# A list schedule that orders a hybrid decoder layer's instructions: port locks, matmul issue times and narrow DMAs enter its model

## The chip, the core and the metric

The kernel runs on one core of a Trainium2 chip. The metric is device time in microseconds (us) of one execution; lower is better. The engines are named as in the profile: PE is TensorE's matmuls and PEld its weight loads, DVE is VectorE, ACT ScalarE, POOL GpSimd, SP the engine whose queue issues all DMAs here.

## The reference

One decoder layer over 2048 tokens of width 1024 in float32, with two groups of heads side by side:

```python
h = rmsnorm(x, norm_w) * (1 + scale) + shift          # scale, shift, gate from c @ w_ada
mq, mk, mv, mo, mz, mi, mf, aq, ak, av, az = split(h @ w_in)
mq, mk = silu(causal_dwconv(mq)), silu(causal_dwconv(mk))
hm = sigmoid(mo) * head_layernorm(mlstm_chunkwise(mq, mk, mv, mi, log_sigmoid(mf))) * silu(mz)
...
logits = q @ k.T + rel_bias[t5_bucket]                # two softmax maps per head, causal
w = softmax(logits_0) - lam * softmax(logits_1)
ha = rmsnorm(w @ v, a_norm_w) * (1 - lam_init) * silu(az)
y = concatenate([hm, ha]) @ w_out
out = rmsnorm(x + gate * y, final_norm_w)
```

The mLSTM group has 4 heads of 256, the attention group 8 heads with two 64-wide query/key maps and 128-wide values.

## The kernel before, in words

Every float32 operand of a large product is split into two parts, `hi` and `lo`, that TensorE reads in its faster float32 form; a product is three matmuls (hi·hi, hi·lo, lo·hi). The split costs one ACT copy (hi) and one subtraction on DVE or POOL (lo). So weights, projected activations, attention weights and the mLSTM state all pass ACT and then DVE or POOL before PE may use them.

`build` (L270) notes the program in this order: `load_x`, `adaln` and `make_h` (normalised tokens), `phase_a` (L721, attention projections of one half of the tokens), `attention` (L798) for the first half, `phase_a` and `attention` for the second, `phase_m` (L940, mLSTM projections), `mlstm` (L1043) for chunks 0 to 7 of 128 tokens, `phase_m` and `phase_zo` for the second half, `mlstm` for chunks 8 to 15, `out_proj` (L1142). Projections, attention maps and states go through DRAM (`dQ`, `dK`, `dV`, `dMK` and so on); all DMAs are issued from SP's queue.

None of these calls issues anything. A `Lane` notes each call in `Program.ops` with the earlier instructions it depends on (`note`, L166). At the end `order` (L195) makes a list schedule: it keeps a modelled time at which each of the five engines is free, gives the engine that is free first the earliest noted instruction whose operands are modelled to be there, and adds the instruction's modelled cost (`cost`, L141) and a latency between engines (`AFTER`). `issue` (L240) then issues everything in that order, so all lines of the profile are L243, and each engine runs its instructions strictly in the order found. The model's times decide nothing but this order. Thus PE gets matmuls of a later projection (`ps_pj`) as filler wherever the model says that the next matmul of the current stage is not ready yet.

```python
if ins[0].dtype == F32R:
    return max(108.0, 3 + n / 2.4)                        # L148, ns
...
if method in ("tensor_scalar", "tensor_copy") and "PSUM" not in str(ins[0].space):
    return 68.0 + n * 0.53                                # L161
```

Three places matter below. In `mlstm`, at the end of a chunk, DVE combines the denominators (`sm`), POOL raises them to the power -1/2 (L1128), DVE normalises the four heads with one `tensor_scalar` each from SBUF to SBUF (`hn`, L1131), and PE transposes each result (L1135). In `attention`, a head begins with two loads of its keys into `Kt`, partitions 0 to 63 and 64 to 127, which may start when the last score matmul (`ps_S`) of the head before has read the old keys. And between the transposes of attention weights (`ps_tr`) and their product with the values (`ps_pv`) stand the ACT copy and the DVE subtraction of the split.

Of the kernel before, what the change touches and what calls it, by code (L numbers as in the profile page):

```python
# [13 lines left out]
PSUM = bass.MemoryType.PSUM  # L14
DRAM = bass.MemoryType.DRAM
# [54 lines left out]
class Lane:  # L70
    """One engine's instruction stream: calls are noted down, not issued."""

# [9 lines left out]
class Program:  # L82
    """Notes the kernel's instructions with what they read and write, then issues them in the
    order of a list schedule: whenever an engine is free it takes the first noted instruction
    whose operands are there."""

# [54 lines left out]
    def cost(self, lane, method, out, ins, kwargs):  # L141
        n = self.width(out)
        if lane == "sync":
            return 530.0
        if lane == "tensor":
            if method == "transpose":
                return 109.0
            if ins[0].dtype == F32R:  # L148
                return max(108.0, 3 + n / 2.4)
            return 2 * max(108.0, 3 + n / 1.2)  # L150
        if lane == "scalar":
            aps = sum(isinstance(kwargs.get(k), bass.AP) for k in ("scale", "bias", "accum_out"))
            return 51.0 + n / 1.2 + 93.0 * aps
        n = max(n, max((self.width(a) for a in ins), default=0))
        if lane == "gpsimd":
            if kwargs.get("op") == ALU.pow:
                return 300.0 + 165.0 * n
            return 150.0 + n * (2.1 if method == "tensor_tensor" else 0.9)
        scalars = [a for a in ins if self.width(a) == 1]
        if method in ("tensor_scalar", "tensor_copy") and "PSUM" not in str(ins[0].space):  # L160
            return 68.0 + n * 0.53  # L161
        if method == "reciprocal":
            return 60.0 + n * 8
        return 68.0 + n * 1.042 + (62.0 if scalars else 0.0)

    def note(self, lane, method, args, kwargs):  # L166
        rest = list(args)
        out = kwargs["out"] if "out" in kwargs else rest.pop(0)
# [4 lines left out]
        deps = set()  # L173
# [15 lines left out]
        if self.hold is not None:  # L189
            deps.add(self.hold)  # L190
        size = 4.0 * self.width(out) * out.shape[0]
        self.ops.append((lane, method, args, kwargs, self.cost(lane, method, out, ins, kwargs),
                         deps, k - self.ahead, size))

    def order(self):  # L195
# [9 lines left out]
        free = {n: 0.0 for n in self.LANES}  # L205
        dma = 0.0
        for k, o in enumerate(ops):
            if left[k] == 0:
                heapq.heappush(soon[o[0]], (0.0, k))
        done = []  # L210
        while len(done) < len(ops):
# [10 lines left out]
            while soon[lane] and soon[lane][0][0] <= best:  # L222
                k = heapq.heappop(soon[lane])[1]
                heapq.heappush(now[lane], (ops[k][6], k))
            k = heapq.heappop(now[lane])[1]
            o = ops[k]
            end = best + o[4] * (2 if lane == "tensor" and best < self.COLD else 1)
            free[lane] = end
            if lane == "sync":
                dma = max(dma, best + 1400.0) + o[7] / 350.0  # L230
                end = dma + 1000.0
# [14 lines left out]
class K:  # L246
# [174 lines left out]

# [1 line left out]
    def ht(self, slot, lo):  # L423
# [5 lines left out]
    def turned(self, n, vecs):  # L429
        """vectors over channels, turned so that channels lie on partitions"""  # L430
        nc = self.nc
# [23 lines left out]
    def adaln(self, g, on_pe):  # L455
        """shift and scale of 256 channels: some of the products on TensorE, the others on VectorE"""
        nc = self.nc
# [30 lines left out]
    def load_x(self, tg):  # L488
        """x of four token tiles, scaled by its reciprocal root mean square"""
        nc = self.nc  # L490
# [41 lines left out]
    def out_gate(self):  # L532
        """the output gate on all partitions, kept in DRAM"""
        nc = self.nc
# [16 lines left out]
    def gate_weights(self):  # L551
        """the gates' columns, beside the last slot of the weight ring"""
        nc = self.nc
# [88 lines left out]

# [1 line left out]
    def fill_w(self, c0, hi, lo, eng=None):  # L644
# [16 lines left out]
    def load_w2(self, c0, *slots):  # L661
        """256 columns in one load: two slots of the ring, or one wide one"""
        nc = self.nc
# [10 lines left out]
    def proj_c(self, w, slot, name):  # L674
        """channel-major block: [128 channels, 512 tokens]"""
        pj = self.psum("pj", name)
        self.proj_k(pj, w, slot, range(KT))
        return pj
# [10 lines left out]
    def proj_t(self, w, slot, j2, name):  # L689
        """token-major block: two tiles of [128 tokens, 256 columns]"""  # L690
        pj = self.psum("pj", name)
        for j in range(2):
            self.proj_r(pj[:, j * 256:(j + 1) * 256], w, slot, 2 * j2 + j)
        return pj
# [81 lines left out]

# [1 line left out]
    def bias_tiles(self):  # L778
# [154 lines left out]

# [1 line left out]
    def stage_m(self):  # L935
# [76 lines left out]

# [1 line left out]
    def mlstm_buffers(self):  # L1014
# [224 lines left out]
```

## Time and profile before

| | |
|---|---|
| time, median of 3 runs | 2996.12 us (2994.66 to 2997.53) |
| profiled execution | span 2997.5 us; it has no time of its own beside the span; the longest of the three times is 2997.53 us |
| busy: PE, PEld | 2849.1 us (95%), 2454.4 us (82%) |
| busy: DVE, ACT, POOL | 1649.4 us (55%), 1351.0 us (45%), 914.4 us (31%) |
| mean granted TensorE clock | 0.980 of full speed |
| DMA | 419.96 MB moved, 140 GB/s in the mean |

The engine table gives the share of the span in which an engine worked; a PE that is 95% busy leaves 148 us of idle time. The windows view cuts this by stage, the waits view says what each idle stretch of PE ended on, and the timeline shows one such place instruction by instruction. A granted clock of 0.50 means 1.2 GHz, of 1.00 means 2.4 GHz.

### The profile page before, as it was taken

What the parts mean: (1) busy time and instruction counts of PE and PEld (TensorE: products, weight loads), DVE (VectorE), ACT (ScalarE), POOL (GpSimd) and SP (SyncE); (2) the same over time, 40 slices, a digit from 0 to 9 for tenths busy, and PEclk for the clock granted to TensorE, in tenths of its full rate; (3) what the DMA queues carried; (4) which work ended last, traced back from release to release, by engine and by line L of the source; (5) the groups of instructions that cost most, each with busy time, mean ns of one, the idle gap of its engine ahead of it and who ended that gap; (6) DMA issues with size and microseconds to landing.
All of it is one profiled execution on the core that took longest, in us unless ns stands there. A gap on an engine that the chain in (4) does not pass through costs nothing.

```text
span 2997.5 us, 43354 instructions
## 1 busy us (share of the span) xinstructions
PE 2849.1 (95%) x16032; PEld 2454.4 (82%) x16032; DVE 1649.4 (55%) x3378; ACT 1351.0 (45%) x3355; POOL 914.4 (31%) x594
## 2 busy tenths in 40 slices
PE   7999999999999999999999999999989889999999
PEld 5878888888888888798887888788788877878887
DVE  6123327776711557766866767866777575232222
ACT  4111325565611455565655656664554454221211
POOL 3112232322312232231221232233544454243332
PEclk9999999999999999999999999999999999999999
DMA  7356667666654632334253335524433444333332
GB/s 257 110 164 231 222 214 218 176 163 176 182 171 123 210 96 87 100 103 115 75 130 84 109 102 190 148 78 123 133 117 98 143 126 150 103 124 115 126 115 97
DMA packets 407539, 419.96 MB, mean 140 GB/s; under 512 B 19540, under 2 KB 348446, under 8 KB 405278
## 3 DMA queue, kind: packets, MB, share of 16 engines
q1 hardware_dynamic: 407326, 417.19, 46.7%
q8 instruction: 126, 2.06, 0.3%
q14 instruction: 87, 0.71, 0.1%
HBM read 280.77 MB, written 136.35 MB: 139 GB/s over the span
## 4 chain that ended last, share of the span: by engine, by line
PE 75%; DVE 10%; DMA 7%; ACT 3%; issue 3%; POOL 2%; SPq 1%; POOLq 0%; DVEq 0%; ACTq 0%
PE ps_pj L243 51%; PE ps_S L243 12%; DVE af L243 7%; PE ps_pv L243 7%; PE ps_tr L243 5%; DMA ar<-dK 3%; ACT af L243 2%; POOL ar L243 1%; ACT ar L243 1%; DVE ar L243 1%; DMA ar<-dQ 1%; SPq L243 1%; DMA af<-in_w_in_dram 1%; DMA ar<-dV 1%; DVE mn L243 1%
## 5 line engine op out<-in xcount | busy, mean ns | idle before, releaser
L243 PE MATMUL ps_pj<-ar 128*128 128x512 f32 (+2 forms) x9936 | 2162.6, 363 | 6.5 <-POOL ar L243 3.1
L243 PEld LDWEIGHTS ps_pj<-ar 128*128 128x128 f32 x9936 | 1648.1, 190 | 268.7 <-issue 5.3
L243 POOL TENSOR_TENSOR ar<-af,ar 128x1024 fp32r<-128x1024 f32 (+3 forms) x308 | 627.9, 2048 | 1068.6 <-ACT ar L243 934.4
L243 PE MATMUL ps_S<-ar 128*128 128x512 f32 (+4 forms) x2096 | 527.6, 357 | 42.3 <-DMA ar<-dK 22.4
L243 ACT ACTIVATE af<-ps_S,nm 128x512 f32<-128x512 f32 (+2 forms) x608 | 386.8, 642 | 141.4 <-DVE nm L243 92.0
L243 ACT ACTIVATE ar<-af 128x1024 fp32r<-128x1024 f32 (+3 forms) x321 | 285.7, 907 | 342.1 <-PE ps_pj L243 201.7
L243 PEld LDWEIGHTS ps_S<-ar 128*128 128x128 f32 x2096 | 351.2, 197 | 91.4 <-issue 33.7
L243 DVE TENSOR_REDUCE mn<-ps_S 128x1 f32<-128x512 f32 (+3 forms) x512 | 297.6, 589 | 146.5 <-PE ps_S L243 143.6
L243 ACT ACTIVATE af<-ps_pj 128x512 f32<-128x512 f32 (+2 forms) x292 | 171.2, 586 | 431.6 <-PE ps_pj L243 385.4
L243 PE MATMUL ps_pv<-ar 128*128 128x256 f32 (+2 forms) x1920 | 319.7, 283 | 20.4 <-DVE af L243 9.2
L243 POOL TENSOR_SCALAR af<-af,rZ,nlam 128x128 f32<-128x128 f32 (+15 forms) x128 | 168.3, 1315 | 529.4 <-DVE rZ L243 445.8
L243 PEld LDWEIGHTS ps_pv<-ar 128*128 128x128 f32 x1920 | 280.5, 190 | 56.7 <-DVE ar L243 16.2
L243 ACT ACTIVATE ar<-ps_tr 128x512 fp32r<-128x512 f32 (+1 forms) x288 | 165.7, 575 | 236.3 <-PE ps_tr L243 226.0
L243 DVE TENSOR_TENSOR ar<-ps_tr,ar 128x512 fp32r<-128x512 f32 (+1 forms) x288 | 188.8, 656 | 113.4 <-ACT ar L243 112.6
L243 DVE SCALAR_TENSOR_TENSOR af<-af,rZ 128x128 f32<-128x128 f32 (+15 forms) x128 | 193.8, 1514 | 27.6 <-POOL af L243 27.3
L243 DVE SCALAR_TENSOR_TENSOR af<-af,cols 128x512 f32<-128x512 f32 x192 | 189.7, 989 | 30.8 <-ACT af L243 28.8
L243 PE MATMUL ps_tr<-ident,af 128*128 128x128 f32 x1115 | 184.8, 277 | 12.9 <-DVE af L243 12.4
L243 DVE TENSOR_TENSOR af<-ps_pj,af 128x512 fp32r<-128x512 f32 (+3 forms) x103 | 66.3, 643 | 186.1 <-ACT af L243 174.7
L243 ACT ACTIVATE af<-af 128x512 f32<-128x512 f32 (+3 forms) x114 | 78.1, 685 | 181.8 <-DVE af L243 176.7
L243 PEld LDWEIGHTS ps_tr<-ident,af 128*128 128x128 f32 x1115 | 134.4, 142 | 26.3 <-DVE af L243 16.5
L243 POOL TENSOR_TENSOR ss<-ss,half 128x2 f32<-128x2 f32 x64 | 48.9, 764 | 337.4 <-DVE ss L243 286.8
L243 DVE TENSOR_TENSOR ps_pj<-ps_pj,af 128x512 f32<-128x512 f32 (+1 forms) x33 | 22.6, 683 | 206.2 <-PE ps_pj L243 206.2
(135 smaller groups left out, 1748.0 us busy)
## 6 DMA issues: line engine op xcount, KB each, us to landing
af<-in_w_in_dram SPq DMA_DIRECT2D x50, 1024.0 KB, 5.1
ar<-dQ SPq DMA_DIRECT2D x128, 256.0 KB, 4.2
af<-in_w_in_dram SPq DMA_DIRECT2D x44, 512.0 KB, 5.0
af<-in_x_dram SPq DMA_DIRECT2D x32, 512.0 KB, 3.8
dQ<-af SPq DMA_DIRECT2D x64, 256.0 KB, 4.8
dK<-af SPq DMA_DIRECT2D x64, 256.0 KB, 3.9
dV<-af SPq DMA_DIRECT2D x64, 256.0 KB, 2.2
dH<-ar SPq DMA_DIRECT2D x32, 512.0 KB, 6.1
```

The lines of the kernel that those rows point to most:

```text
L243: getattr(getattr(nc, lane), method)(*args, **kwargs)
```

## The change

Only the schedule's model changes; the noted instructions, their number and their data are the same. Four edits: a float32-form matmul of n columns costs 13 + n/2.4 ns in place of 3 + n/2.4; a DMA with 64 or fewer partitions on the SBUF side counts 1/0.55 times its bytes against the modelled 350 bytes per ns; a new function `locks` marks the instructions that hold a port pair common to DVE and POOL (POOL's that read SBUF; DVE's copies and `tensor_scalar` from SBUF to SBUF, and DVE's with two wide SBUF inputs); and `order` lets a marked instruction start only when the other engine's last marked one has ended: the engine is put off to that time, and nothing else is taken for it before.

```diff
-                return max(108.0, 3 + n / 2.4)
+                return max(108.0, 13 + n / 2.4)
...
+    def locks(self, lane, method, out, ins):
+
+        near = [a for a in ins if str(a.space).split(".")[-1] == "SB"]
+        if lane == "gpsimd":
+            return bool(near)
+        if lane != "vector":
+            return False
+        if method in ("tensor_scalar", "tensor_copy"):
+            return "PSUM" not in str(ins[0].space) and "PSUM" not in str(out.space)
+        if method in ("tensor_tensor", "scalar_tensor_tensor", "tensor_tensor_scan"):
+            return sum(self.width(a) > 1 or self.width(out) == 1 for a in near) > 1
+        return False
...
+        if lane == "sync" and min(a.shape[0] for a in [out] + ins if "DRAM" not in str(a.space)) <= 64:
+            size /= 0.55
         self.ops.append((lane, method, args, kwargs, self.cost(lane, method, out, ins, kwargs),
-                         deps, k - self.ahead, size))
+                         deps, k - self.ahead, size, self.locks(lane, method, out, ins)))
...
+        port, holder = 0.0, None
...
-            k = heapq.heappop(now[lane])[1]
+            k = now[lane][0][1]
             o = ops[k]
+            if o[8] and holder != lane and port > best:
+                free[lane] = port
+                continue
+            heapq.heappop(now[lane])
             end = best + o[4] * (2 if lane == "tensor" and best < self.COLD else 1)
             free[lane] = end
+            if o[8]:
+                port, holder = end, lane
```

All engines' orders move. Three places follow; L243 is the line of the issue before, L265 the same line now.

PE's queue where head 2 of the second `attention` begins, before. `ps_S_133` in the first row are the last matmuls that read the old keys, `ps_S_134` in the last row the first that read the new ones; `ps_pj` is projection filler, 512 columns each:

```order
L243 MATMUL ps_S_133<-ar 128x512 x2
L243 MATMUL ps_pj_139<-ar 128x512
L243 MATMUL ps_pv<-ident,af 128x128 x2
L243 MATMUL ps_pj_139<-ar 128x512 x11
L243 MATMUL ps_pj_140<-ar 128x512 x5
L243 MATMUL ps_pv<-ident,af 128x128 x2
L243 MATMUL ps_pj_140<-ar 128x512 x19
L243 MATMUL ps_pj_139<-ar 128x512 x5
L243 MATMUL ps_S_134<-ar 128x512 x2
```

The same place now; between the last read of the old keys and the first row here stand two more `ps_pj` of 512 columns and two `ps_pv` of 256:

```order
L265 MATMUL ps_pv<-ar 128x128 x3
L265 MATMUL ps_tr<-ident,af 128x128
L265 MATMUL ps_pj_139<-ar 128x512 x6
L265 MATMUL ps_pv<-ident,af 128x128 x2
L265 MATMUL ps_pj_139<-ar 128x512 x17
L265 MATMUL ps_pj_140<-ar 128x512 x3
L265 MATMUL ps_pv<-ident,af 128x128 x2
L265 MATMUL ps_pj_140<-ar 128x512 x21
L265 MATMUL ps_tr<-ident,af 128x128 x3
L265 MATMUL ps_pj_139<-ar 128x512 x6
L265 MATMUL ps_pv<-ar 128x256
L265 MATMUL ps_S_134<-ar 128x512 x2
```

Before, 41 filler matmuls and 4 transposes stood between the two; now 55 filler matmuls, 8 transposes and 6 `ps_pv` do.

PE's queue at the end of mLSTM chunk 10, before. The `ps_pv` rows end the chunk's numerators; `ps_S<-ident` are the transposes of `hn`, two per head:

```order
L243 MATMUL ps_pv<-ar 128x258 x2
L243 MATMUL ps_pj_139<-ar 128x512 x11
L243 MATMUL ps_S_134<-ident,af 128x128 x2
L243 MATMUL ps_S_135<-ident,af 128x128 x2
L243 MATMUL ps_pj_139<-ar 128x512 x3
L243 MATMUL ps_S_136<-ident,af 128x128 x2
L243 MATMUL ps_S_133<-ident,af 128x128 x2
```

The same place now:

```order
L265 MATMUL ps_pv<-ar 128x258 x2
L265 MATMUL ps_pj_139<-ar 128x512 x21
L265 MATMUL ps_pj_140<-ar 128x512 x15
L265 MATMUL ps_tr<-af,ar 128x128
L265 MATMUL ps_S_134<-ident,af 128x128 x2
L265 MATMUL ps_S_135<-ident,af 128x128 x2
L265 MATMUL ps_tr<-af,ar 128x128 x3
L265 MATMUL ps_S_136<-ident,af 128x128 x2
L265 MATMUL ps_S_133<-ident,af 128x128 x2
```

The transposes of the first two heads moved from behind 11 filler matmuls to behind 36.

POOL's queue at the same place, before. `sm` is the power that `hn` waits for, `ar<-af,ar 128x1024` the subtraction of a split weight, `128x8x128` that of the next chunk's queries:

```order
L243 TENSOR_TENSOR ar<-af,ar 128x516
L243 TENSOR_TENSOR sm_187<-sm_187,half 128x4
L243 TENSOR_TENSOR ar<-af,ar 128x1024
L243 AFFINE_SELECT af<-af 128x512
L243 TENSOR_TENSOR ar<-af,ar 128x8x128
```

The same place now:

```order
L265 TENSOR_TENSOR ar<-af,ar 128x516
L265 TENSOR_TENSOR ar<-af,ar 128x1024
L265 AFFINE_SELECT af<-af 128x512
L265 TENSOR_TENSOR sm_187<-sm_187,half 128x4
L265 TENSOR_TENSOR ar<-af,ar 128x8x128
```

The weight's subtraction and the mask went from behind the power to ahead of it.

## Rows read from the trace of the kernel before

**Rows 1.** The page, engines: busy us (share of the span) xinstructions.

```profile
PE 2849.1 (95%) x16032; PEld 2454.4 (82%) x16032; DVE 1649.4 (55%) x3378; ACT 1351.0 (45%) x3355; POOL 914.4 (31%) x594
```

**Rows 2.** Windows: stretch, length, busy PE, PEld, DVE, ACT, POOL, PEclk, DMA share, GB/s.

```profile
448.00:850.00 402.00, 378.06 (x2314) 332.04 (x2314) 276.20 (x868) 233.83 (x742) 116.80 (x112) 0.98 0.69 187
1050.00:2065.00 1015.00, 974.28 (x5747) 849.26 (x5746) 718.56 (x1372) 589.97 (x1589) 264.53 (x137) 0.98 0.39 109
2065.00:2535.00 470.00, 422.92 (x2675) 377.32 (x2674) 329.80 (x613) 242.93 (x537) 223.26 (x141) 0.95 0.42 127
```

**Rows 3.** Waits of PE, whole span: us in total, times, longest us.

```profile
PE ps_S L243 <- DVE af L243: 35.4, 21, 4.1
PE ps_S L243 <- DMA ar<-dK: 22.4, 9, 3.9
PE ps_tr L243 <- DVE af L243: 15.6, 10, 3.8
PE ps_pv L243 <- DVE ar L243: 8.5, 13, 1.9
...
PE ps_S L243 <- ACT af L243: 3.4, 7, 1.0
```

**Rows 4.** Timeline at the end of mLSTM chunk 10: start us, us, engine, line, operation.

```profile
2406.91 0.40 PE L243 MATMUL ps_pv<-ar 128*128 128x258 f32 x2
...
2407.15 2.72 PE L243 MATMUL ps_pj<-ar 128*128 128x512 f32 x11
...
2408.92 2.36 POOL L243 TENSOR_TENSOR ar<-af,ar 128x1024 fp32r<-128x1024 f32 x1
2408.99 5.77 DVE L243 TENSOR_SCALAR af<-af,mvt,sm 128x256 f32<-128x256 f32 x4 [0.29 <-POOL sm L243]
...
2411.58 0.99 PE L243 MATMUL ps_S<-ident,af 128*128 128x128 f32 x4 [1.70 <-DVE af L243]
...
2411.90 2.39 POOL L243 TENSOR_TENSOR ar<-af,ar 128x1024 fp32r<-128x1024 f32 x1
...
2414.50 1.11 PE L243 MATMUL ps_S<-ident,af 128*128 128x128 f32 x4 [1.22 <-DVE af L243]
```

**Rows 5.** The tile mvt: engine, operation, count, duration ns min/median/max, first and last start.

```profile
L243 DVE TENSOR_SCALAR af<-af,mvt,sm x64: 399/413/2439, 2091.4 to 2532.3; 128x256 f32<-128x256 f32 x64
```

**Rows 6.** Groups by form: operation, names, shapes, count | busy us, mean ns | idle before.

```profile
L243 DVE SCALAR_TENSOR_TENSOR af<-af,cols 128x512 f32<-128x512 f32 x192 | 189.7, 989 | 30.8 <-ACT af L243 28.8
...
L243 DVE TENSOR_SCALAR af<-af,mvt,sm 128x256 f32<-128x256 f32 x64 | 56.4, 920 | 14.2 <-POOL sm L243 11.4 <-PE ps_S L243 2.6
...
L243 DVE SCALAR_TENSOR_TENSOR af<-af,ps_pj 128x512 f32<-128x512 f32 x64 | 43.7, 684 | 136.6 <-ACT af L243 136.4
```

**Rows 7.** Groups by form, the split of attention weights and the score path.

```profile
L243 ACT ACTIVATE af<-ps_S,nm 128x512 f32<-128x512 f32 x400 | 275.8, 693 | 127.9 <-DVE nm L243 87.9 <-PE ps_tr L243 37.0 <-DVE af L243 1.7
...
L243 DVE TENSOR_TENSOR ar<-ps_tr,ar 128x512 fp32r<-128x512 f32 x224 | 153.4, 685 | 69.6 <-ACT ar L243 68.9
L243 ACT ACTIVATE ar<-ps_tr 128x512 fp32r<-128x512 f32 x224 | 134.5, 600 | 202.4 <-PE ps_tr L243 192.1 <-PE ps_pv L243 5.3 <-DVE nm L243 3.3
```

**Rows 8.** Windows: out_proj alone, then two stretches of low clock; columns as in rows 2.

```profile
2775.00:2850.00 75.00, 75.00 (x332) 62.10 (x331) 17.50 (x30) 15.81 (x31) 24.46 (x21) 1.00 0.41 130
...
1253.40:1260.20 6.80, 5.54 (x15) 4.61 (x16) 2.23 (x4) 0.00 (x0) 0.00 (x0) 0.50 0.56 144
2359.30:2366.10 6.80, 4.47 (x16) 3.78 (x17) 4.24 (x5) 3.06 (x10) 2.82 (x2) 0.50 0.31 87
```

**Rows 9.** The chain of waits where head 2 of the second attention begins: start us, us, what.

```profile
1240.37 0.47 PE ps_S L243 x2
...
1241.50 13.02 DMA ar<-dK
...
1254.66 3.11 PE ps_S L243 x8
```

**Rows 10.** The chain of waits, whole span: the shortest key load of the second attention that ends a wait.

```profile
1109.11 11.67 DMA ar<-dK
```

## The prediction

> **What bounds the kernel now.** Read the engine table first. PE is busy for 95% of the span, DVE for 55%, ACT 45%, POOL 31% [rows 1]: PE sets the end, and the kernel can only lose PE's idle time (2997.5 - 2849.1 = 148 us) and the time in which PE works at a low clock. The changed schedule issues the same instructions, so this is all that it can give or take. The windows by stage come second: PE idles 24 us of 402 in the first attention, 41 of 1015 in the second, 47 of 470 in the mLSTM stage [rows 2], in all 112 of the 148. These stages also show a granted clock of 0.98, 0.98 and 0.95, where out_proj alone shows 1.00 [rows 2, 8].
>
> The waits of PE say third what the idle time ended on [rows 3]. The largest entry, 35.4 us in 21 waits, is `ps_S` on DVE `af`, the transposes of `hn`. The next, 22.4 us in 9 waits, is `ps_S` on the loads of keys. Both have one cause to be seen in a timeline: too few filler matmuls stand in PE's queue for what the result really takes. At the end of chunk 10 PE runs 11 fillers, done near 2409.9, and then stands for 1.70 and once more for 1.22 us, since DVE's four `tensor_scalar` take 5.77 us [rows 4]. They take 399 ns at best and 2439 at worst [rows 5], 920 in the mean [rows 6], while the schedule counted 204 (68 + 256 x 0.53). The long ones lie beside POOL's subtractions of 2.36 and 2.39 us [rows 4].
>
> A second row tells the same of another form: a DVE operation over 512 columns with both wide inputs in SBUF takes 989 ns, the one with an input in PSUM 684 [rows 6]. So DVE and POOL stand in each other's way, and the old model did not know it.
>
> **The change part by part.** *The port locks.* A chunk's four `tensor_scalar` now cost, in the model, what POOL holds them up for, and the schedule answers with filler. At chunk 10, 36 matmuls stand where 11 stood. One takes 75 us / 332 = 0.226 us [rows 8], so the cover is 8.1 us in place of 2.5. The transposes of the first two heads began 4.3 us after the last `ps_pv` had ended (2406.91 + 0.40 to 2411.58), those of the last two 7.2 us after it [rows 4]: 8.1 us covers both. But in POOL's queue a subtraction of 2.4 us and a mask now stand ahead of the power, and the next chunk's subtraction right behind it: if the power comes later by some 3 us and one POOL operation still gets in, the need is near 8.8 us and 0.7 us a chunk stay. With 16 chunks (x64 in rows 5 is four heads each), 11 us would stay at worst, 0 at best; I take 8. Saved: 35.4 - 8 = **27 us**.
>
> Here a rule speaks against the change. *The rows show* that the one who came first kept the other out: the power ended, POOL's subtraction began at 2408.92, DVE's `tensor_scalar` at 2408.99, and the first transposes came only at 2411.58, after POOL's 2.36 us [rows 4]. The Trainium skill, "SBUF — State Buffer", section "Who interferes with whom", says that the order of issue, not the shape of the operation, decides who blocks, and for the whole instruction. The rows bear that out. The schedule grants the port by modelled times, so a power that ends a little sooner or later on the chip gives the port to another than it planned. If nothing else changed, one more subtraction of 2.39 us would have to be waited for where it was not planned; the sum then keeps more of the 35.4 us. I put this among the rivals, not into the sum, since the new cover already holds one such operation.
>
> *DMAs on 64 partitions.* The two loads of a head's keys take 13.02 us in the chain of waits; PE's last read ended at 1240.84 and its next score matmul came at 1254.66, 13.8 us later [rows 9]. The shortest such load that ended a wait took 11.67 [rows 10], a need of some 12.5. Before, 41 fillers gave 9.3 us and four transposes a little more. Now 55 fillers give 12.4 us, and 14 short matmuls, taken at half a filler each, 1.6: 14.0 us. That covers both needs, one of them by a hair. The loads are issued from the same place of SP's queue right after the last read (0.66 us later), so the later place of PE does not delay them. Of 22.4 us I leave 4. Saved: **18 us**. Bounds: 0, should the loads wait for other DMAs, and 22.4.
>
> *Clock.* The three stages lack 0.02 x 402 + 0.02 x 1015 + 0.05 x 470 = 52 us of granted clock [rows 2]. In two stretches at 0.50, that is 1.2 GHz, PE was busy 5.54 and 4.47 of 6.8 us [rows 8], 74%, so 0.74 x 52 = 38 us were lost by work at the lower level. The first of these stretches lies just behind the wait for keys of rows 9, the second in the mLSTM stage; the clock fell after PE had stood idle. If the long waits go, most dips go: I take three quarters, **29 us** (bounds 0 and 38).
>
> *Matmul issue.* 13 + 512/2.4 = 226 ns is what the row shows [rows 8]; the old 216 counted each filler 10 ns short, so every cover was in truth 4.6% longer than planned. This spare goes. Where it was the margin, small waits grow: `ps_pv` on DVE `ar` (8.5 us in 13 waits) and `ps_S` on ACT `af` (3.4 in 7) [rows 3]. I let both double: **12 us lost**. Below, nothing. Above: the 224 splits of attention weights need at least 0.600 + 0.685 = 1.3 us, the 400 score tiles 0.7 us each [rows 7]; if three times that is covered (an estimate; queues and semaphores lie between), the spare is 17 and 9 fillers of 10 ns, in all 224 x 0.17 + 400 x 0.09 = 74 us, lost only if every place binds.
>
> *New places.* A list that is ordered anew will have waits where none were. The nearest row of a wait that no part above touches is `ps_tr` on DVE `af`, 15.6 us [rows 3]; I add two thirds of that, **10 us lost** (bounds 0 and 15.6). DVE's and POOL's longer queues cost nothing as long as their busy shares of 55% and 31% leave room; the cover, if it went, would show as `ps_pj` waiting on POOL.
>
> **The sum.** 27 + 18 + 29 - 12 - 10 = 52 us off the profiled execution: 2997.5 - 52 = 2945 us. That execution's span is 1.4 us above the median of the three runs, too little to correct for. Against 2996.1 this is 1.7% less. About 0.2%, 6 us, is what a measurement of this kernel can tell from no change.
>
> **The rivals.** *The waits go whole.* All of 35.4, 22.4 and 38 us go and the losses cancel against smaller waits elsewhere: 2997.5 - 96 = 2902 us. For it: the new covers exceed the needs at each place that I show. Against: the key loads are covered by a hair.
>
> *The port goes to another.* By the rule above, one unplanned subtraction a chunk gets in between the heads' `tensor_scalar`; the second pair of transposes follows the first with almost no cover of its own. Of 2.39 us, 0.9 is spare (8.1 against 7.2), so 1.5 x 16 = 24 us come back, and with them some of the clock, say 10: 2945 + 34 = 2979 us. For it: POOL's two operations within one set of `tensor_scalar` [rows 4]; against: the next subtractions in POOL's queue need the next chunk's PE work first.
>
> *The spare was needed: slower.* The 4.6% of each cover made up for what the model prices too low on ACT and DVE. Then all 224 splits and 400 score tiles become short by their spare, 74 us in place of 12: 2945 + 62 = 3007 us. It decides from the point at which nearly nine tenths of these places bind (52 us of gain against 62 more). Against: 13 and 7 such waits today [rows 3] among 624 places.
>
> *Nothing comes of it.* The waits change places and the sum stays within 6 us of the old time, 2996 us: the `tensor_scalar` wait as long as now, only later. Against: PE's total of idle time then has to stay although its two largest entries have cover.
>
> **How the numbers follow.** My forecast has 0.52, the waits that go whole 0.18, the port rival 0.15, no change 0.06, the slower one 0.09. Faster by over 0.2%: 0.52 + 0.18 + 0.15 = 0.85; same 0.06; slower 0.09. The range reaches from a little under the second case, 2895, to a little over the third, 2985; outside lie the last two and the tails, under 0.2.
>
> **What would show it.** In the changed profile: `ps_S` on DVE `af` at 8 us or less, `ps_S` on the key loads at 4 or less, the granted clock of the mLSTM stage at 0.98 or more and of both attentions at 0.99; PE's idle time near 110 us. `ps_pv` on DVE `ar` would stand near 17 us, `ps_S` on ACT `af` near 7. `ps_S` on DVE `af` at 20 us or more would mean the port rival; hundreds of short waits on ACT and DVE in both attentions, with few long ones left, the slower one. An idle PE that shrank without the clock's recovery would make my third term wrong.

## The result, and the profile after

The changed kernel takes **2870.07 us** (median of 4 runs, 2868.54 to 2871.9) against 2996.82 us of the kernel before (4 runs, 2994.66 to 3003.0): a ratio of 0.9577 with a 95% interval of 0.9562 to 0.9591. It is 127 us faster, where 51 were forecast, and lies below the range. The profiled execution has a span of 2866.8 us, 130.7 less than before.

First the engine table of the kernel after (as rows 1):

```profile
PE 2801.2 (98%) x16032; PEld 2432.4 (85%) x16032; DVE 1620.4 (57%) x3378; ACT 1348.1 (47%) x3355; POOL 903.6 (32%) x594
```

The instructions are as many as before. PE's idle time fell from 148.4 to 65.6 us (82.8 less), its busy time from 2849.1 to 2801.2 (47.9 less), together the 130.7. The rows of the stretches in which the granted clock was 0.50 (1.2 GHz) say what part of the busy time went with the clock. Before there are 25 of them, now 7; their sums read, before and after (the first number is their length, the second PE's busy time in them, in us):

```profile
sum 119.41, PE 101.69 PEld 88.71 DVE 53.58 ACT 37.77 POOL 20.69; mean PE 4.07 PEld 3.55 DVE 2.14 ACT 1.51 POOL 0.83
```

```profile
sum 36.94, PE 32.13 PEld 28.87 DVE 20.70 ACT 13.69 POOL 15.17; mean PE 4.59 PEld 4.12 DVE 2.96 ACT 1.96 POOL 2.17
```

If half of PE's time in them is what the low level costs (an estimate, from 1.2 against 2.4 GHz), that cost was 50.8 us and is 16.1: the clock gave back 35 of the 47.9 us. The other 13 us fit with restarts, though no run separates them. PE stood idle for more than 20 ns 118 times before and 51 times now, and by the start and end of every matmul in the two traces, the matmul that ends such a stretch adds 0.22 to 0.23 us more to the busy time than its form does in the median, half of its time at the low clock left out (512 columns of `ps_pj` before, at full clock: 499 ns in the mean of ten, against a median of 231). That makes 26.5 us before and 11.8 now, 15 less.

The windows of the kernel after, over the stretches of [rows 2]:

```profile
448.00:850.00 402.00, 396.67 (x2487) 350.94 (x2486) 276.93 (x861) 239.57 (x747) 121.64 (x112) 1.00 0.71 194
1050.00:2065.00 1015.00, 1003.37 (x6120) 886.96 (x6119) 740.91 (x1434) 612.13 (x1632) 279.47 (x156) 1.00 0.42 119
2065.00:2535.00 470.00, 451.78 (x2671) 398.18 (x2670) 296.11 (x534) 233.80 (x487) 235.77 (x139) 0.98 0.44 134
```

PE's idle time in them went from 24, 41 and 47 us to 5, 12 and 18, and the granted clock from 0.98, 0.98 and 0.95 to 1.00, 1.00 and 0.98. So more of the gain lies in the attentions, 48 us of idle time, than in the mLSTM stage, 29 us, of which the forecast spoke first.

The waits of PE in the kernel after (as rows 3: us in total, times, longest us):

```profile
PE ps_S L265 <- DVE af L265: 8.6, 5, 4.4
...
PE ps_tr L265 <- DVE af L265: 6.7, 5, 1.7
PE ps_pj L265 <- DVE af L265: 6.7, 5, 2.4
...
PE ps_pv L265 <- DVE ar L265: 2.5, 2, 1.4
...
PE ps_pv L265 <- DVE af L265: 2.0, 3, 0.7
...
PE ps_S L265 <- DMA ar<-dQ: 1.0, 1, 1.0
...
PE ps_S L265 <- ACT af L265: 0.4, 1, 0.4
```

Three entries of the same view of the kernel before that the forecast had no term for:

```profile
PE ps_pv L243 <- DVE af L243: 11.0, 8, 4.7
...
PE ps_S L243 <- issue: 8.2, 5, 3.6
...
PE ps_S L243 <- DMA ar<-dQ: 5.8, 5, 2.2
```

Against [rows 3], `ps_S` on DVE fell by 26.8 us, and no entry for the loads of keys (22.4) is left. But the rest fell too: `ps_tr` on DVE from 15.6 to 6.7, `ps_pv` on DVE `af` from 11.0 to 2.0, `ps_pv` on DVE `ar` from 8.5 to 2.5, `ps_S` on ACT from 3.4 to 0.4, on `dQ` from 5.8 to 1.0, and the wait on issue is gone. These six make 40 us, of which the forecast saw none go. Two of them, the wait on issue and the one on `dQ`, have to do with the loads on 64 partitions: the issue waits stand at heads' beginnings in the place of a key wait (the longest, 3.6 us, ends at 1510.35 us in the row of the other heads' key waits at 1254.66, 1382.39 and 1635.63), so I count 22.4 + 8.2 = 30.6 us of waits for the loads of keys before.

Two groups by form of the kernel after, the first two of [rows 6]:

```profile
L265 DVE SCALAR_TENSOR_TENSOR af<-af,cols 128x512 f32<-128x512 f32 x192 | 169.7, 893 | 13.8 <-ACT af L265 12.8
...
L265 DVE TENSOR_SCALAR af<-af,mvt,sm 128x256 f32<-128x256 f32 x64 | 35.0, 588 | 16.4 <-POOL sm L265 9.1 <-PE ps_S L265 7.2
```

Both take less time themselves, 893 in place of 989 ns and 588 in place of 920 in the mean: in the new order GpSimd holds these up less.

### The profile page after: what moved, and what is told of

It reads as the page before. It is cut to its first block, busy times and chain, and to the rows that moved or that the text cites. A ratio compares the mean times of both kernels' runs of the same rounds, so it can differ in the third digit from the quotient of the medians.

```text
span 2866.8 us, 43387 instructions
## 1 busy us (share of the span) xinstructions
PE 2801.2 (98%) x16032; PEld 2432.4 (85%) x16032; DVE 1620.4 (57%) x3378; ACT 1348.1 (47%) x3355; POOL 903.6 (32%) x594
## 4 chain that ended last, share of the span: by engine, by line
PE 88%; DMA 4%; DVE 4%; ACT 1%; issue 1%; POOL 1%; SPq 0%; POOLq 0%; DVEq 0%; ACTq 0%
PE ps_pj L265 62%; PE ps_S L265 12%; PE ps_pv L265 8%; PE ps_tr L265 5%; DVE af L265 2%; DMA ar<-dV 1%; ACT af L265 1%; POOL ar L265 1%; DVE ar L265 0%; ACT ar L265 0%; DMA af<-dMQ 0%; DMA af<-in_w_in_dram 0%; DVE mn L265 0%; DMA ar<-dH 0%; DMA ar<-dMK 0%
## 5 line engine op out<-in xcount | busy, mean ns | idle before, releaser
L265 PE MATMUL ps_pj<-ar 128*128 128x512 f32 (+2 forms) x9936 | 2149.1, 361 | 5.6 <-DVE af L265 2.2
L265 PEld LDWEIGHTS ps_pj<-ar 128*128 128x128 f32 x9936 | 1635.9, 188 | 266.0 <-issue 5.3
L265 POOL TENSOR_TENSOR ar<-af,ar 128x1024 fp32r<-128x1024 f32 (+3 forms) x308 | 620.5, 2026 | 1018.8 <-ACT ar L265 900.2
L265 PE MATMUL ps_S<-ar 128*128 128x512 f32 (+4 forms) x2096 | 506.4, 347 | 1.8 <-DMA ar<-dQ 1.0
L265 ACT ACTIVATE af<-ps_S,nm 128x512 f32<-128x512 f32 (+2 forms) x608 | 385.8, 641 | 148.4 <-DVE nm L265 91.3
L265 ACT ACTIVATE ar<-af 128x1024 fp32r<-128x1024 f32 (+3 forms) x321 | 285.1, 908 | 354.7 <-PE ps_pj L265 233.1
L265 PEld LDWEIGHTS ps_S<-ar 128*128 128x128 f32 x2096 | 342.5, 192 | 41.2 <-ACT af L265 2.0
L265 DVE TENSOR_REDUCE mn<-ps_S 128x1 f32<-128x512 f32 (+3 forms) x512 | 297.6, 589 | 129.5 <-PE ps_S L265 127.0
L265 ACT ACTIVATE af<-ps_pj 128x512 f32<-128x512 f32 (+2 forms) x292 | 170.9, 586 | 405.2 <-PE ps_pj L265 347.8
L265 POOL TENSOR_SCALAR af<-af,rZ,nlam 128x128 f32<-128x128 f32 (+15 forms) x128 | 164.8, 1287 | 551.2 <-DVE rZ L265 404.8
L265 PE MATMUL ps_pv<-ar 128*128 128x256 f32 (+2 forms) x1920 | 318.6, 280 | 10.0 <-DMA ar<-dV 3.9
L265 PEld LDWEIGHTS ps_pv<-ar 128*128 128x128 f32 x1920 | 281.0, 189 | 40.9 <-DMA ar<-dV 5.5
L265 ACT ACTIVATE ar<-ps_tr 128x512 fp32r<-128x512 f32 (+1 forms) x288 | 165.7, 575 | 195.1 <-PE ps_tr L265 179.5
L265 DVE TENSOR_TENSOR ar<-ps_tr,ar 128x512 fp32r<-128x512 f32 (+1 forms) x288 | 189.1, 657 | 116.3 <-ACT ar L265 114.4
L265 DVE SCALAR_TENSOR_TENSOR af<-af,rZ 128x128 f32<-128x128 f32 (+15 forms) x128 | 190.0, 1484 | 33.2 <-POOL af L265 32.3
L265 PE MATMUL ps_tr<-ident,af 128*128 128x128 f32 x1115 | 183.2, 274 | 7.2 <-DVE af L265 6.7
L265 DVE SCALAR_TENSOR_TENSOR af<-af,cols 128x512 f32<-128x512 f32 x192 | 169.7, 893 | 13.8 <-ACT af L265 12.8
L265 DVE TENSOR_TENSOR af<-ps_pj,af 128x512 fp32r<-128x512 f32 (+3 forms) x103 | 66.2, 643 | 176.3 <-ACT af L265 174.1
L265 PEld LDWEIGHTS ps_tr<-ident,af 128*128 128x128 f32 x1115 | 133.0, 140 | 18.9 <-DVE af L265 9.2
L265 DVE TENSOR_TENSOR ps_pj<-ps_pj,af 128x512 f32<-128x512 f32 (+1 forms) x33 | 22.6, 683 | 205.4 <-PE ps_pj L265 205.4
L265 ACT ACTIVATE af<-af 128x512 f32<-128x512 f32 (+3 forms) x114 | 77.9, 684 | 129.1 <-DVE af L265 121.4
L265 POOL TENSOR_TENSOR ss<-ss,half 128x2 f32<-128x2 f32 x64 | 50.9, 795 | 244.8 <-DVE ss L265 214.4
```

Source lines behind the costliest of these rows:

```text
L265: getattr(getattr(nc, lane), method)(*args, **kwargs)
```

## The experiments

All kernels issue the same instructions as the kernel after; each edit alters the schedule's model, and so the order. Each time stands against runs of the kernel before on the same chip (medians 2995.2 to 2997.2 us).

**Each part alone, and each part left out.** The two prices and the test of the port locks are set back, in the combinations of the table:

```diff
-                return max(108.0, 13 + n / 2.4)
+                return max(108.0, 3 + n / 2.4)       # without the matmul price
...
-            size /= 0.55
+            size /= 1.0                              # without the price of 64 partitions
...
-            if o[8] and holder != lane and port > best:
+            if False and o[8] and holder != lane and port > best:   # without the port locks
```

e1, locks alone: 

> The port locks alone; matmuls priced 3 + n/2.4 and DMAs on 64 partitions at their bytes, as before. Theory A (each part removes its own waits, and the parts add up): the hn wait (ps_S on DVE af) falls from 35.4 to about 9 us and the clock of the mLSTM stage recovers, key waits stay near 22 us and the attentions' clock stays 0.98: about 2930 us. Theory B (the issue time of matmuls is what puts the modelled times right; without it locks and DMAs fall at the wrong moments): no more than a third of the gain, 2960 us or more. Theory C (any new order would have done as well): no tie between the part left in and the waits that go.

e2, matmul price alone: 

> The matmul issue time alone, 13 + n/2.4; no locks, DMAs as before. Theory A: the cover of every wait shrinks by 4.6%, so small waits on ACT and DVE grow while hn and key waits stay: 2997 to 3010 us. Theory B: waits of all kinds shrink, 2950 us or less.

e3, DMA price alone: 

> The DMA price alone. Theory A: the waits of ps_S on key and query loads (28 us) fall to 5 or less and the clock of both attentions goes to 0.99 or 1.00, hn waits stay at 35: about 2950 us. Theory B: 2975 us or more.

e4, no locks: 

> The change without the locks (matmul issue time and DMA price stay). Theory A: hn waits stay near 35 us or grow a little, key waits gone: 2940 to 2955 us. Theory B: nearer to the changed kernel, 2900 us or less.

e5, no matmul price: 

> Locks and DMA price, matmuls at the old 3 + n/2.4. The runs so far: locks alone -86 us, DMA price alone -42, matmul issue time alone +53, DMA and matmul -10, all three -127. Theory A' (parts add up, and the thinner cover of the right matmul price costs its 53 us here too): 2815 to 2825 us. Theory D (with the locks the waits are priced right, so the cover that the matmul price takes away is spare only; it costs next to nothing beside them): 2860 to 2880 us.

e6, no DMA price: 

> Locks and matmul issue time, DMAs at their bytes. Theory A': 2995 - 86 + 53 = 2962 us. Theory D: the change less the DMA price's 42 us, 2905 to 2920 us, with key waits (ps_S on DMA dK) of 20 us or more and hn waits under 10.

| kernel | locks | matmul | DMA | us, median (range) | ratio (95%) |
|---|---|---|---|---|---|
| e1 | x | | | 2908.69 (2904.50 to 2910.95) | 0.9717 (0.9701 to 0.9733) |
| e2 | | x | | 3048.57 (3044.82 to 3056.80) | 1.0190 (1.0169 to 1.0211) |
| e3 | | | x | 2953.37 (2948.81 to 2957.09) | 0.9867 (0.9846 to 0.9888) |
| e4 | | x | x | 2985.07 (2980.34 to 2991.85) | 0.9971 (0.9958 to 0.9983) |
| e5 | x | | x | 2907.81 (2906.93 to 2909.14) | 0.9712 (0.9697 to 0.9727) |
| e6 | x | x | | 2930.26 (2928.49 to 2931.70) | 0.9786 (0.9771 to 0.9801) |
| after | x | x | x | 2870.07 (2868.54 to 2871.90) | 0.9577 (0.9562 to 0.9591) |

The parts do not add up. The locks bring 86 us alone and 115 beside the other two; the DMA price 42 alone, 1 beside the locks, 60 beside both. The matmul price costs 53 us alone, 32 beside the DMA price and 22 beside the locks, and brings 38 beside both. Its sign turns, and that is the point to explain. Of the readings named in the expectations only e3's sum of parts came true; e1, e2, e4, e5 and e6 came out in none of their ranges.

What the locks end is read from the waits of PE in e4, which lacks them alone, and in e1, which has them alone:

```profile
PE ps_S L265 <- DVE af L265: 42.1, 24, 5.1
PE ps_tr L265 <- DVE af L265: 23.4, 15, 3.8
```

```profile
PE ps_S L265 <- DVE af L265: 2.3, 2, 1.7
```

In e1 `ps_tr` and `ps_pv` on DVE `ar` have no entry, and `ps_pv` on DVE `af` reads 1.5 us.

The keys' term is read from one line. In the waits of PE of e1, then of e6, which both lack the DMA price:

```profile
PE ps_S L265 <- DMA ar<-dK: 26.0, 10, 3.7
```

```profile
PE ps_S L265 <- DMA ar<-dK: 29.1, 10, 4.5
```

In e3 and e5, which have it, the entry is absent, and in e4 it reads 1.0 us. The wait of `ps_S` on issue goes with it: 8.1 us in e1, 9.5 in e6 and 23.1 in e2, none in e3, e4 and e5. So that price is what ends these waits; in the four kernels without it, before, e1, e2 and e6, the two entries make 31 to 39 us.

**Which operations have to hold the port.** e8 leaves VectorE's operations with two inputs in SBUF out of the rule, e12 those with one:

```diff
-        if method in ("tensor_tensor", "scalar_tensor_tensor", "tensor_tensor_scan"):      # e8
-            return sum(self.width(a) > 1 or self.width(out) == 1 for a in near) > 1        # e8
-        if method in ("tensor_scalar", "tensor_copy"):                                     # e12
-            return "PSUM" not in str(ins[0].space) and "PSUM" not in str(out.space)        # e12
```

> The whole change, but DVE's operations with two wide SBUF inputs (tensor_tensor, scalar_tensor_tensor) are not taken to hold the port; copies and tensor_scalar still are. If hn's tensor_scalar are what the locks gain by: 2870 to 2885 us. If the 989 ns convolution steps and the attention weights' scalar_tensor_tensor matter as well: 2900 us or more, with ps_tr on DVE af back at 15 us.

> The whole change, but the port rule knows only VectorE's operations with two SBUF inputs; those with one (tensor_scalar, tensor_copy) are planned as if free of it. If the two kinds cost apart from each other: the wait of ps_S on DVE for the layer norm's products comes back to 25 to 40 us, the attentions' waits stay as with the whole change, 2895 to 2915 us. If either kind alone keeps GpSimd's work off VectorE's: 2870 to 2880 us.

e8 took 2959.85 us (2954.09 to 2964.91; 0.9885, 0.9864 to 0.9905), e12 2884.81 (2881.44 to 2888.15; 0.9629, 0.9603 to 0.9656). Without any lock it is 2985 (e4), with both kinds 2870: marked alone, the two-input kind brings 100 of the 115 us, the one-input kind 25. The waits of PE show where. In the second attention (1050 to 2065 us), e8 and then e12:

```profile
PE ps_tr L263 <- DVE af L263: 19.5, 10, 3.8
PE ps_pv L263 <- DVE ar L263: 13.0, 10, 2.9
```

```profile
PE ps_pv L263 <- DVE ar L263: 2.2, 2, 1.5
...
PE ps_tr L263 <- DVE af L263: 0.7, 1, 0.7
```

The first entry is the `scalar_tensor_tensor` that joins the two maps of attention weights (tile `rZ`). In the tile view of `rZ`, 27.0 us of `ps_tr` waits end on it in e8, 12.4 before, 6.7 in the kernel after and 2.9 in e12. It follows a POOL `tensor_scalar` on the other map, and POOL's further work may run beside it. The longest one before shows it:

```profile
1504.55 4.57 POOL L243 TENSOR_TENSOR ar<-af,ar 128x2048 fp32r<-128x2048 f32 x1
...
1504.63 6.64 DVE L243 SCALAR_TENSOR_TENSOR af<-af,rZ 128x2048 f32<-128x2048 f32 x1 [2.31 <-POOL af L243]
```

POOL's subtraction began 0.08 us sooner; the shortest of the eight joins of this size takes 2.34 us, so this one was held up for some 4.3. In the tile view of `rZ` (duration ns min/median/max), first before, then after:

```profile
L243 DVE SCALAR_TENSOR_TENSOR af<-af,rZ x128: 341/1418/6641, 451.3 to 2028.4; 128x128 f32<-128x128 f32 x8, 128x256 f32<-128x256 f32 x8, 128x384 f32<-128x384 f32 x8, 128x512 f32<-128x512 f32 x8
```

```profile
L265 DVE SCALAR_TENSOR_TENSOR af<-af,rZ x128: 341/1408/6712, 446.3 to 1959.5; 128x128 f32<-128x128 f32 x8, 128x256 f32<-128x256 f32 x8, 128x384 f32<-128x384 f32 x8, 128x512 f32<-128x512 f32 x8
```

It is hardly faster than it was, and its longest is still over 6.6 us. What changed is that PE waits less for it, 6.7 in place of 12.4 us: the plan now gives it cover. The joins are not all of the 100 us, though. From e4 to e12 PE's idle time falls from 144 to 75 us; `ps_tr` on DVE `af` accounts for 20 of that, and `ps_S` on DVE `af`, the layer norm's products, for 26 (42.1 to 15.7).

Part of e12's expectation failed: I expected the layer norm's wait back at 25 to 40 us, and between 2065 and 2760 us the entry of `ps_S` on DVE reads 11.8 in 8 waits; the `tensor_scalar` themselves take 731 ns there, against 588 in the kernel after and 920 before. Marking the two-input kind alone takes most of this wait away too. The time fell between the two ranges that I had named.

One rival is left: the locks also spend more projection matmuls on covers. No run gives away as much cover without the port rule, by a flat surcharge on VectorE's operations for example, so it is not shown apart what the rule brings beyond longer covers. Against this rival speak e8 and e12, by which it matters which operations are marked, and e13 below, which spends 146 more matmuls on covers than the kernel after and is 3 us faster.

**The matmul price: how much, and where.** e7 and e13 to e16 put another number in place of 13; e9 and e10 let the price change where the mLSTM phase begins, ahead of its first `load_h` (`nc.late = 1`):

```diff
-                return max(108.0, 13 + n / 2.4)
+                return max(108.0, (13 if self.late else 3) + n / 2.4)      # e9; e10: (3 if self.late else 13)
```

> The whole change, with 12 + n/2.4 in place of 13; two thirds of PE's places in the order hold another instruction. Theory C (the gain is a lucky order among many): a time that may lie 30 us or more from 2870. Theories A' and D (the model's prices decide, not the single order): within 10 us of 2870.

> Port locks and 64-partition price as in the change; the matmul price is 13 + n/2.4 ns only for the work noted from the mLSTM phase's first layer norm on, and 3 + n/2.4 before it. In this order 250 projection matmuls are left behind the last mLSTM chunk (0 with the low price everywhere, 368 with the whole change). If the matmul price gains by keeping projection work as cover until the out-projection's weights are in, this comes near the whole change: 2870 to 2885 us, no wait of ps_pj on ACT above 3 us. If the right price gains everywhere by better order, about half of the 38 us is lost: 2885 to 2905 us.

> The reverse: 13 + n/2.4 ns up to the mLSTM phase, 3 + n/2.4 from there on. No projection matmul is left behind the last mLSTM chunk in this order. If cover kept to the end is what the matmul price buys: 2900 to 2912 us, with ps_pj waiting on ACT for 10 us or more ahead of the out-projection. If the price gains in the attentions: 2870 to 2885 us.

> The whole change with 9 + n/2.4 ns for a matmul. In this order 222 projection matmuls are left behind the last mLSTM chunk (0 at 3 ns, 368 at 13 ns). If what counts is that projection work lasts until the out-projection's weights are in: 2870 to 2885 us and no wait of ps_pj on ACT over 3 us. If the true price counts: about 2890 us, 4 of the 10 ns being missed. If the 38 us were luck: anything from 2870 to 2910.

> The whole change with 11 + n/2.4 ns for a matmul; 247 projection matmuls are left. Projection work that lasts: 2865 to 2882 us. The true price: some 2878 us. Luck: anything from 2870 to 2910.

> The whole change with 15 + n/2.4 ns for a matmul; 322 projection matmuls are left. Projection work that lasts: 2865 to 2882 us. The true price, with too thin a cover from 13 ns on: some 2878 us. Luck: anything from 2870 to 2910.

> The whole change with 17 + n/2.4 ns for a matmul; 327 projection matmuls are left. Projection work that lasts: 2865 to 2885 us. The true price: 2885 us or more, each cover being 2 percent short, with more waits on DVE and ACT in both attentions than the 9 us of the change. Luck: anything from 2870 to 2910.

The third column counts, in the order in which PE is given its work, the projection matmuls behind the last one of the last mLSTM chunk:

| kernel | price, ns | projection matmuls left | us, median (range) | ratio (95%) |
|---|---|---|---|---|
| e5 | 3 | 0 | 2907.81 (2906.93 to 2909.14) | 0.9712 (0.9697 to 0.9727) |
| e13 | 9 | 222 | 2866.85 (2865.34 to 2867.21) | 0.9570 (0.9551 to 0.9589) |
| e14 | 11 | 247 | 2859.60 (2858.20 to 2864.30) | 0.9550 (0.9529 to 0.9570) |
| e7 | 12 | 281 | 2879.34 (2878.21 to 2879.80) | 0.9615 (0.9598 to 0.9632) |
| after | 13 | 368 | 2870.07 (2868.54 to 2871.90) | 0.9577 (0.9562 to 0.9591) |
| e15 | 15 | 322 | 2864.14 (2860.89 to 2868.07) | 0.9563 (0.9542 to 0.9583) |
| e16 | 17 | 327 | 2874.42 (2873.77 to 2877.80) | 0.9600 (0.9576 to 0.9623) |
| e9 | 3, then 13 | 250 | 2869.17 (2868.14 to 2869.78) | 0.9577 (0.9552 to 0.9602) |
| e10 | 13, then 3 | 0 | 2884.48 (2882.71 to 2889.99) | 0.9631 (0.9604 to 0.9659) |

From 9 to 17 ns there is no slope: six orders lie between 2859.6 and 2879.3 us. The value that the trace shows is not the best one: 4 ns less is 3 us faster, 4 ns more 4 us slower. e13, e14 and e15 came out 1 to 5 us below the lowest range that I had named for them. The step is between 3 and 9 ns, and there the projection work runs out. In the waits of PE of e5, then of e10:

```profile
PE ps_pj L265 <- ACT ar L265: 16.4, 5, 5.5
```

```profile
PE ps_pj L266 <- ACT ar L266: 20.8, 6, 5.4
```

No kernel of the table in which projection work is left has this entry among its waits. These are the first matmuls of `out_proj`, which wait until its weights are loaded and split: in the chain of waits of e5 from 2510 to 2560 us, 31% is the loads of `w_out`, 25% POOL's half of the split, 12% ACT's. The windows of e5 at that place:

```profile
2470.00:2510.00 40.00, 33.22 (x185) 29.08 (x183) 29.70 (x52) 22.80 (x42) 21.57 (x11) 0.91 0.54 177
2510.00:2550.00 40.00, 16.33 (x44) 10.33 (x44) 9.77 (x12) 12.19 (x19) 17.58 (x10) 0.60 0.43 134
2550.00:2590.00 40.00, 37.27 (x138) 29.27 (x139) 10.19 (x14) 7.38 (x15) 10.36 (x9) 0.85 0.30 92
```

PE stands idle for 23.7 of 40 us, and the clock, at 0.60 there, is not wholly back in the next window either (0.85). In the kernel after the windows just past its last chunk read:

```profile
2430.00:2470.00 40.00, 40.00 (x174) 32.42 (x174) 8.67 (x8) 12.11 (x15) 19.26 (x8) 1.00 0.45 142
2470.00:2510.00 40.00, 37.81 (x163) 29.98 (x161) 14.85 (x15) 16.22 (x22) 9.56 (x5) 1.00 0.35 115
```

Projection work is a stock. A matmul that is counted 10 ns short makes each cover 4.6% longer than the plan wants, and what is spent there is missing at the end. The windows from 0 to 2430 and from 2430 to 2760 us say it in numbers: PE idles 53 and 33 us in e5, 33 and 38 in e10, 56 and 2 in the kernel after. e5 thus loses 28 us of idle time against the kernel after; PE is busy for 12.6 us longer (2813.8 against 2801.2), which makes the 40.6 between the spans. Of the 33 us at its end, 16.4 are the entry above and 12.6 the layer norm's products of the last chunks, which have no cover left either. The time of e10, 2884.5 us, lies in the range that I had named for a gain in the attentions; its wait of 20.8 us on ACT is the sign of the other reading. The same sum explains why it lost only 14 us of the 38 where I expected 30 or more: its low price late, in the mLSTM stage, did buy shorter waits there (1.7 us idle from 2065 to 2430 us, 16 in the kernel after).

The stock runs out only where the locks spend it. Counted in the same way, 447 projection matmuls are left in the kernel before and in e3, both at 3 ns, and 471 in e2 and e4; with the locks and 3 ns 64 are left in e1 and none in e5. 64 are too few: e1 has 11.7 us of `ps_pj` on ACT. So without the locks the dearer matmul has nothing to save.

Why the price then costs 53 us alone: with the ports and the key loads unpriced, covers are too short, and I take it that the spare had made up for part of that. In the waits of PE of e2:

```profile
PE ps_S L265 <- DVE af L265: 43.5, 24, 4.1
PE ps_S L265 <- issue: 23.1, 7, 4.5
PE ps_S L265 <- DMA ar<-dK: 14.6, 6, 3.9
PE ps_pv L265 <- DVE ar L265: 13.1, 12, 3.2
```

The first is 8 us above [rows 3], the next two together 7 us above the 30.6 of the kernel before, the last 5 us; the clock of its first attention stands at 0.94. The time is that of the rival "the spare was needed", but its sign, hundreds of short waits on ACT and DVE, is not there: these are few and long. Beside the locks alone it is similar: from e1 to e6 the price ends the 11.7 us on ACT, but `ps_S` on DVE grows from 2.3 to 10.4 and `ps_tr` on DVE from nothing to 7.7.

**More prices.** e11 is the change with four more costs set to what its own trace shows:

```diff
-            return 51.0 + n / 1.2 + 93.0 * aps
+            near = 42.0 if "PSUM" not in str(ins[0].space) else 0.0
+            return 51.0 + n / 1.2 + 93.0 * aps + near
...
-                return 300.0 + 165.0 * n
-            return 150.0 + n * (2.1 if method == "tensor_tensor" else 0.9)
+                return 380.0 + 158.0 * n
+            return 150.0 + n * 2.1 if method == "tensor_tensor" else 290.0 + n * 0.89
...
-            return 68.0 + n * 0.53
+            return 68.0 + n * 0.53 + (120.0 if len(scalars) > 1 and n > 1 else 0.0)
```

> The whole change, and four more prices set to what its trace shows: ScalarE with an SBUF input 42 ns dearer, GpSimd power 380 + 158 n/128 ns, GpSimd tensor_scalar 290 + 0.89 n ns, VectorE tensor_scalar with two scalars 120 ns dearer. 250 projection matmuls are left behind the last mLSTM chunk. If the plan still loses by wrong prices: 2850 to 2865 us, with the waits on DVE and ACT in the attentions below 20 us together. If what is left is not a matter of prices: 2865 to 2880 us.

It took 2855.16 us (2854.43 to 2855.83; 0.9530, 0.9500 to 0.9560), the fastest of all, 142 us under the kernel before. The sign that I had named, waits on DVE and ACT in the attentions below 20 us, does not decide: they make 11 us in e11 and 11 in the kernel after. And over the whole span waits on DVE are left, in the waits of PE of e11:

```profile
PE ps_pj L266 <- DVE af L266: 7.1, 6, 2.0
PE ps_S L266 <- DVE af L266: 6.9, 5, 1.7
PE ps_tr L266 <- DVE af L266: 4.3, 2, 3.0
```

It beats both kernels, and by 15 us the changed one. But six values of the matmul price that should be about as good spread over 20 us, and the best of them, e14, is 4.4 us away. So it is not shown that the four prices are the reason.

## Why the prediction was wrong

**The direction and the places named were right.** *The layer norm's products:* 27 us forecast, 26.8 measured, the entry at 8.6 where 8 was named. *Key loads:* 18 forecast, 22.4 measured, which was the upper bound, and the 8.2 us on issue besides; the later need that was "covered by a hair" was covered. e1 and e6 against e3 and e5 tie these waits to the DMA price. PE's idle time, for which the text named 110 us (its own sum makes 125), stands at 65.6.

**The step that failed first is "New places".** It took `ps_tr` on DVE `af` for "a wait that no part above touches" and charged 10 us for new waits. But 12.4 of its 15.6 us are the join of the attention weights, a VectorE operation with two inputs in SBUF beside GpSimd's work. The new `locks` marks it, and the row that proves the hold-up of such operations, 989 against 684 ns [rows 6], was read in the prediction without being followed to the operations that it concerns. The locks were priced at one place, the four `tensor_scalar` of a chunk; e8 and e12 show that the kind to which these belong brings 25 us when it is marked alone, and the other kind 100. In place of a loss of 10, `ps_tr` and `ps_pv` on DVE `af` fell by 18 us. That the locks did this, e1 shows: with them alone the two read none and 1.5 us, in e3 and e4, without them, 15.9 and 6.6, 23.4 and 9.9. A further 13 us, issue and `dQ`, had no term either; the 8.2 on issue went with the DMA price. New waits there are, but small: `ps_pj` on DVE grew by 3.6, from 3.1.

**The second is "Matmul issue".** "This spare goes" was right, and "nothing" as the lower bound was not. The forecast let `ps_pv` on DVE `ar` and `ps_S` on ACT double, 12 us; they fell by 9. With the price alone they did grow (e2: 8.5 to 13.1 and 3.4 to 5.2); beside the locks they do not, since the first of them is gone with the locks alone (e1). So the loss was read for a kernel without the other parts. Beside both other parts the price brings 38 us, for which there was no term: it keeps the stock of projection work from being spent too soon (e9, e13 to e16 against e5). A cover was looked at by itself, without asking what its matmuls are taken from.

**The third is PE's busy time.** It fell by 47.9 us where 29 were forecast under "Clock", with 38 as the most. The mechanism held and the size of this term was about right: with the waits gone the attentions show 1.00, and the low stretches gave back 35 us. (The busy share in all 25 of them was 85%, 101.69 of 119.41 us, not the 74% of the two that were read.) What the sum lacked is a term for restarts: 118 idle stretches became 51, and with them some 15 us of busy time went.

**The rivals.** "The waits go whole", 2902 us, was nearest, and still 32 us too slow, since it too had no gain at the joins, on issue and by restarts. "The port goes to another" did not decide: a `tensor_scalar` still takes up to 2495 ns in the tile view of the kernel after, against 2439 before [rows 5], so the one who comes second is still kept out, but the wait behind it is 8.6 us and not 20. The rule of the Trainium skill ("SBUF — State Buffer", "Who interferes with whom"), that the order of issue decides who blocks, agrees with this trace (the subtraction at 1504.55 and the join at 1504.63 us), and did not speak against the change: a plan need not prevent a hold-up, only expect it. "The spare was needed" names the time of e2 (3048.6 us) without its sign, and did not come true beside the locks and the DMA price. "Nothing comes of it" is nearest to e4, the change without its locks, at 2985.

Open is what in the orders makes the 20 us between prices of 9 and 17 ns; I take it for the luck of a list schedule and have not shown it place by place.

## What to carry to other kernels

When a change gives a planner a new rule, list every operation that the rule marks, look for each one's wait in the trace, and only then call a wait untouched. Filler is a stock: ask of each cover not only whether it is long enough, but what will be missing at the end. And judge a schedule's price by several values of it, since one reordering of the same work moved this kernel by up to 20 us.

## What was unexpected in the hardware

A wait costs PE more than the time for which it stands idle. The busy time for the same 16032 matmuls runs from 2863.4 us (e2, clock 0.94 in its first attention) through 2849.1 (before) to 2798.5 (e11), 65 us between the ends, without an instruction more or less. By the same working as for the result, the low clock accounts for some 45 of them (119.7 us busy at 0.50 in e2, 29.2 in e11), and restarts for some 18 (125 idle stretches against 46). And a hold-up need not get shorter to cost less: the longest join of attention weights takes 6.6 us before and 6.7 after, some 4.3 of them beside a GpSimd subtraction of 4.6 us, while PE's waits on the joins fell from 12.4 to 6.7 us.
